# Norms of both MLPs and of the odd mixer summed row by row on ScalarE; their transposes and weight-sum transfers moved at the MLP entry

## The chip, the core and the metric

The kernel runs on one core of one Trainium2 chip. The metric is the device time of one execution in microseconds (us), as the median of several runs. The work is shared by TensorE (matmuls and transposes, PE below), VectorE (DVE), ScalarE (ACT), GpSimd (POOL), and the DMA queues that SyncE (SP) and GpSimd issue. TensorE writes its results into PSUM banks; `acc` names the banks of the projections and `aux` those of smaller jobs.

## The reference

A sequence of 512 rows with 1024 features goes through two layers, each a mixer and an MLP. Each of the four steps has its own RMS norm:

```python
def _rmsnorm(x, g):
    y = x * rsqrt(mean(x * x, axis=-1) + 1e-6)
    return y * g

def _mlp(x, g, w1, w2):                 # 1024 -> 4096 -> 1024
    return square(relu(_rmsnorm(x, g) @ w1)) @ w2

x = x + even_mixer(x)                   # window and neighbourhood attention
x = x + _mlp(x, ...)                    # "first MLP" below
x = x + odd_mixer(x)                    # q, k, v, g = rmsnorm(x) @ w_in; retention
x = x + _mlp(x, ...)                    # "second MLP" below
```

All inputs are float32.

## The kernel before, in words

**Products.** Every float32 operand of a matmul is split into a high and a low part (`whi`, `wlo` of a weight chunk, `xh`, `xl` of the residual times the norm's gain). A product is three matmuls: high by high, low by high, high by low; in a projection these are lines 177, 178 and 179 (`proj_a`) or 252 to 254 (`proj_b`). ScalarE casts the high part (line 158 for weights, 296 for the residual), VectorE subtracts for the low part (159 and 300). A chunk of weights holds four of the eight feature blocks, so a projection takes a new chunk at feature blocks 0 and 4.

**The residual.** It lies with features on the partitions, as eight tiles `xT` of 128 features by 512 rows. In the MLPs it is also wanted with rows on the partitions: `turn` transposes it (line 1346, 16 transposes of 128x128 for each half of the features) and ScalarE copies the result into the `rows` tiles. At the end of the first MLP `back` (line 1367) transposes it again, and `leave` copies it into `xT` for the odd mixer.

**The norm.** The norm's factor for a row of the sequence is applied behind the product, so a projection can start before the factor is known. The class `Norm` gets it so: ScalarE squares each `xT` tile (lines 321 and 324), the eight squares are added into `sqsum` (line 325, on GpSimd for the first MLP and the odd mixer, on VectorE for the second MLP), the sum is split into `sum_h` (cast, ScalarE, 339) and `sum_l` (VectorE, 340), and two matmuls with a tile of ones (341 and 342) sum over the partitions. `scales` then transposes the result `nv` into a column (four tiny transposes, line 1409) for the MLPs; `rows` and `cols` make from it the factor along the rows (`rstd_b`) for the q and k of the odd mixer and a column for its v.

**The MLP.** The second matmul of the MLP runs as a Strassen scheme, a hand-made schedule (`stream`) whose operands are sums of weight blocks. Its entry (`enter`) computes the first hidden blocks as four projections, called (0,0), (0,1), (1,0) and (1,1) below, 48 matmuls each. Between them stand other jobs: `scales`, `combine` (sums for the Strassen scheme from the residual), `ask` (which issues the transfers of the weight sums: a plain load on SP's queue, and where two blocks are to be added an accumulating transfer on GpSimd's queue, line 1099) and `turn`. The order of instructions on an engine is fixed when the kernel is built, and each engine runs its own in that order.

Of the kernel before, what the change touches and what calls it, by code (L numbers as in the profile page):

```python
# [32 lines left out]
def hybrid_encoder_kernel(  # L33
# [59 lines left out]
    rstd_c = consts.tile([P, 8], F32, name="rstd_c")  # L93

    consts.tile([P, 80], F32, name="filler")
# [66 lines left out]
    def proj_a(w, r0, nk, c0, xs, evac):  # L162
# [10 lines left out]
        for k, m in [(k, m) for k in range(nk) for m in range(2)]:  # L173
            hi, lo = weights(k - k % 4)
# [132 lines left out]
    class Norm:  # L307


        def __init__(self, vec):  # L310
            self.vec = vec
            self.xg = new_xg()
            self.sum = stat.tile([P, S], F32, tag="sqsum", name="sqsum")
            self.n = 0
# [4 lines left out]
        def square(self, d):  # L319
# [8 lines left out]
            self.n += 1  # L328

        def add(self, d):  # L330
            split_gain(self.xg[d], xT[d], self.gain(d))
            self.square(d)

        def squares(self):

            pb = aux()
            h = stat.tile([P, S], F32R, tag="rstd_b", name="sum_h")
            l = stat.tile([P, S], F32R, tag="sq", bufs=2, name="sum_l")
            nc.scalar.copy(h, self.sum)
            V.tensor_tensor(l, self.sum, h[:].bitcast(F32), op=ALU.subtract)  # L340
            mm(pb, ones_r, h, start=True, stop=False)
            mm(pb, ones_r, l, start=False, stop=True)
            v = stat.tile([P, S], F32, tag="sq", bufs=2, name="nv")
            V.tensor_scalar(v, pb, 1.0 / D, RMS_EPS, op0=ALU.mult, op1=ALU.add)
            return v

        def rows(self):

            v = self.squares()
            r = stat.tile([P, S], F32, tag="rstd_b", name="rstd_b")  # L350
            t = stat.tile([P, S], F32, tag="sq", bufs=2, name="nt")
            act(t, v, AF.Ln)
            act(r, t, AF.Exp, scale=-0.5)
# [1470 lines left out]
```

## Time and profile before

| what | value |
|---|---|
| runs | 1318.51, 1322.91, 1318.40 us; median 1318.51 us |
| profiled execution | 1322.95 us, of which the span is 1321.2 us |
| busy in the span | PE 1292.3 us (98%), DVE 1011.0 (77%), ACT 791.6 (60%), POOL 150.3 (11%) |
| DMA | 168.83 MB, 128 GB/s over the span |

The span is the time from the first to the last instruction that the profiler saw; the run's own time is 1.75 us longer. Busy is the sum of an engine's instructions. The times of the trace are counted from the span's start: the first MLP's entry runs from about 221 to 290 us, the odd mixer begins at about 566 us, the second MLP's entry at about 979 us. In a timeline the start of a matmul is followed by its duration; matmuls overlap, so what a matmul costs is the distance from one start to the next. In brackets stands how long the engine was idle before it, and which instruction released it.

### The profile page before, as it was taken

The page shows a single profiled execution, that of the slowest core. Times are in us where ns is not written, and L with a number is a line of the kernel's source. Part 1 is how long each engine was busy: PE and PEld are TensorE (multiplying, and loading weights), DVE is VectorE, ACT ScalarE, POOL GpSimd, SP SyncE. Part 2 cuts the span into 40 slices and gives each one's busy share as a digit, 9 for nine tenths or more (in the row PEclk, how much of TensorE's full clock was granted, in tenths as well). Part 3 has the DMA queues.
Part 4 walks back from the last instruction along what each step waited for, and adds up shares of the span by engine and source line. Part 5 has one row for each costly group of instructions (what it writes and reads, how often), then busy time and mean ns, then how long its engine had stood idle before and what let it go on. Part 6 is the DMA issues. An engine that isn't in the chain of part 4 may idle for free.

```text
span 1321.2 us, 18591 instructions
## 1 busy us (share of the span) xinstructions
PE 1292.3 (98%) x6954; PEld 1117.5 (85%) x6954; DVE 1011.0 (77%) x1568; ACT 791.6 (60%) x1308; POOL 150.3 (11%) x143
## 2 busy tenths in 40 slices
PE   7999999899999999999999999999999999999998
PEld 6888978688989989878888888888888889898997
DVE  5788887859797997976847647646678697979888
ACT  4789875665766757544645345345457657566573
POOL 0222431301011101030000000000000101101100
PEclk9999999999999999989999999999999999999999
DMA  5323322648688686232131332232236587867862
GB/s 167 86 78 89 99 65 80 183 125 199 175 197 199 163 203 177 65 95 94 49 96 48 96 96 64 80 96 80 64 97 191 140 200 185 194 170 176 219 152 80
DMA packets 147243, 168.83 MB, mean 128 GB/s; under 512 B 10817, under 2 KB 113233, under 8 KB 147153
## 3 DMA queue, kind: packets, MB, share of 16 engines
q1 hardware_dynamic: 120000, 134.89, 33.1%
q0 software_dynamic: 21408, 29.38, 13.7%
q10 hardware_dynamic: 5744, 3.37, 0.9%
q8 instruction: 55, 0.90, 0.3%
q14 instruction: 36, 0.29, 0.1%
HBM read 164.47 MB, written 3.15 MB: 127 GB/s over the span
## 4 chain that ended last, share of the span: by engine, by line
PE 89%; DVE 5%; ACT 2%; DMA 1%; POOL 1%; issue 1%; ACTq 0%; SPq 0%; DVEq 0%; POOLq 0%
PE acc L179 8%; PE acc L178 8%; PE acc L177 8%; PE acc L1338 7%; PE acc L1336 7%; PE acc L1337 7%; PE acc L1324 5%; PE acc L1325 5%; PE acc L1326 5%; PE acc L252 3%; PE acc L254 3%; PE acc L253 3%; PE aux L1634 1%; PE aux L1635 1%; PE aux L1636 1%; PE aux L1338 1%
## 5 line engine op out<-in xcount | busy, mean ns | idle before, releaser
L158 ACT CAST whi<-wraw 128x1024 fp32r<-128x1024 f32 (+2 forms) x115 | 112.0, 974 | 175.5 <-PE acc L178 89.9
L159 DVE TENSOR_TENSOR wlo<-wraw,whi 128x1024 fp32r<-128x1024 f32 (+2 forms) x106 | 123.4, 1164 | 92.1 <-ACT whi L158 90.7
L177 PE MATMUL acc<-xh,whi 128*128 128x512 f32 x400 | 157.5, 394 | 1.4 <-DVE xT L867 1.4
L178 PE MATMUL acc<-xl,whi 128*128 128x512 f32 x400 | 157.4, 393 | 0.3 <-DVE xl L300 0.3
L179 PE MATMUL acc<-xh,wlo 128*128 128x512 f32 x400 | 157.3, 393 | 0.0
L1128 ACT CAST whi<-sraw 128x1024 fp32r<-128x1024 f32 x94 | 98.6, 1051 | 66.1 <-PE acc L1338 27.8
L1134 DVE TENSOR_TENSOR wlo<-sraw,whi 128x1024 fp32r<-128x1024 f32 x94 | 114.9, 1222 | 20.1 <-ACT whi L1128 19.8
L1099 POOL DMA_DIRECT2D sraw<-in_w_mlp_out_dram x32 | 38.5, 1226 | 735.2 <-DMA sraw<-in_w_mlp_out_dram 510.8
L177 PEld LDWEIGHTS acc<-xh,whi 128*128 128x128 f32 x400 | 75.9, 190 | 17.8 <-DVE xT L867 1.8
L178 PEld LDWEIGHTS acc<-xl,whi 128*128 128x128 f32 x400 | 76.1, 190 | 16.2 <-DVE xl L300 0.7
L179 PEld LDWEIGHTS acc<-xh,wlo 128*128 128x128 f32 x400 | 75.9, 190 | 16.2 <-DVE wlo L159 0.2
L1324 PE MATMUL acc<-uh,whi 128*128 128x256 f32 x256 | 73.0, 285 | 0.2
L1325 PE MATMUL acc<-ul,whi 128*128 128x256 f32 x256 | 72.4, 283 | 0.0
L1326 PE MATMUL acc<-uh,wlo 128*128 128x256 f32 x256 | 72.4, 283 | 0.0
L1128 ACT CAST shi<-sraw 128x1024 fp32r<-128x1024 f32 x46 | 48.3, 1050 | 31.1 <-PE acc L1338 10.7
L1134 DVE TENSOR_TENSOR slo<-sraw,shi 128x1024 fp32r<-128x1024 f32 x46 | 56.2, 1222 | 9.2 <-ACT shi L1128 9.0
L252 PE MATMUL acc<-whi,xh 128*128 128x512 f32 x160 | 63.2, 396 | 0.0
L253 PE MATMUL acc<-wlo,xh 128*128 128x512 f32 x160 | 62.8, 394 | 0.0
L254 PE MATMUL acc<-whi,xl 128*128 128x512 f32 x160 | 62.7, 393 | 0.0
L202 PE MATMUL acc<-wlo,xh 128*128 128x384 f32 (+1 forms) x160 | 52.6, 329 | 0.0
L201 PE MATMUL acc<-whi,xh 128*128 128x384 f32 (+1 forms) x160 | 52.6, 331 | 0.0
L203 PE MATMUL acc<-whi,xl 128*128 128x384 f32 (+1 forms) x160 | 52.1, 327 | 0.0
(359 smaller groups left out, 3900.7 us busy)
## 6 DMA issues: line engine op xcount, KB each, us to landing
sraw<-in_w_mlp_out_dram SPq DMA_DIRECT2D x48, 512.0 KB
wraw<-in_w_in_o_dram SPq DMA_DIRECT2D x48, 512.0 KB
wraw<-in_w_mlp_in_dram SPq DMA_DIRECT2D x40, 512.0 KB
sraw<-in_w_mlp_in_dram SPq DMA_DIRECT2D x36, 512.0 KB
sraw<-in_w_mlp_out_dram POOLq DMA_DIRECT2D x32, 512.0 KB, 8.7
wraw<-in_w_mlp_out_dram SPq DMA_DIRECT2D x32, 512.0 KB
sraw<-in_w_mlp_in_dram POOLq DMA_DIRECT2D x24, 512.0 KB, 7.9
wraw<-in_w_out_o_dram SPq DMA_DIRECT2D x16, 512.0 KB
```

Of the source, the lines that this page charges most:

```text
L158: nc.scalar.copy(hu, used)
L159: eng.tensor_tensor(lu, used, hu.bitcast(F32), op=ALU.subtract)
L177: mm(ps[m], hi[:, k % 4, cs], xh, start=k == 0, stop=False)
L178: mm(ps[m], hi[:, k % 4, cs], xl, start=False, stop=False)
L179: mm(ps[m], lo[:, k % 4, cs], xh, start=False, stop=k == nk - 1)
L252: mm(o, lh, hi[:, k, :ncols], start=kb + k == 0, stop=False)
L1128: nc.scalar.copy(h, self.weight(k))
L1134: V.tensor_tensor(l, self.weight(k), h.bitcast(F32), op=ALU.subtract)
L1324: mm(o, h[:, i, cs], bh, start=st, stop=False, skip_group_check=True)
L1325: mm(o, h[:, i, cs], bl, start=False, stop=False, skip_group_check=True)
L1326: mm(o, l[:, i, cs], bh, start=False, stop=i == 3, skip_group_check=True)
L1338: mm(o, bl[:, i, cs], h[:, i], start=False, stop=end, skip_group_check=True)
```

## The change

The squares are taken from the `rows` tiles, which have the rows of the sequence on the partitions: `act(junk, rows, Square, accum_out=...)` is one ScalarE instruction that writes the squares to a place nobody reads and sums them along the row into one column of `tok_ss` (128 partitions, 4 blocks of rows, 2 halves of the features). So `sqsum`, its adds, the split, the two ones-matmuls and the transposes of `nv` are gone. `mean_square` adds the two halves and scales them (two VectorE instructions on 128x4). For the MLPs `scales` needs a reciprocal and a negation on 128x4 more. For the odd mixer a function `deviations`, called from the middle of the first q projection (before feature block 4), takes Ln and Exp on ScalarE and four refining VectorE instructions on 128x4, spreads the result over 128x512 (`wide`), transposes it four times (line 1489 of the kernel after) and copies it into `rstd_b`; v takes the column directly.

To have the rows early enough, `turn(0)` stands after projection (0,1) and `turn(1)` after (1,0), where they stood after (1,0) and after (1,1); `turn(1)`'s row copies, which were spread over the first four steps of `stream`, follow it at once. `scales` moves from after (0,0) to after (1,0). The first `ask` moves from after (0,0) to after (0,1), and the limits of the asks change.

```diff
-            if self.n == 0:
-                act(self.sum, xT[d], AF.Square)
-            else:
-                sq = stat.tile([P, S], F32, tag="sq", bufs=2, name="sq")
-                act(sq, xT[d], AF.Square)
-                (V if self.vec == V_MLP + 8 else G).tensor_tensor(
-                    self.sum, self.sum, sq, op=ALU.add
-                )
...
+    def mean_square():
+
+        v = tok_v
+        V.tensor_tensor(v, tok_ss[:, :, 0], tok_ss[:, :, 1], op=ALU.add)
+        V.tensor_scalar(v, v, 1.0 / D, RMS_EPS, op0=ALU.mult, op1=ALU.add)
+        return v
...
+        def square(self, t, half, junk):
+            act(junk, self.rows[t, half], AF.Square, accum_out=tok_ss[:, t, half : half + 1])
...
                     if (u, f) == (0, 0):
-                        self.scales()
                         self.combine(0)
                         self.combine(1)
-                        self.ask(-99, -8)
                     elif (u, f) == (0, 1):
                         self.combine(2)
-                        self.ask(-8, -5)
+                        self.turn(0)
+                        self.ask(-99, -6)
                     elif (u, f) == (1, 0):
                         self.combine(3)
-                        self.ask(-5, -2)
-                        copy = self.turn(0)
-                        for t in range(NB):
-                            copy(t)
+                        self.turn(1)
+                        self.ask(-6, -2)
+                        self.scales()
                         self.high(0)
                         self.low(0)
                     else:
                         self.ask(-2, 0)
-                        copy = self.turn(1)
-                        for k, t in enumerate((2, 3, 0, 1)):
-                            self.early.setdefault(k, []).append(lambda t=t: copy(t))
...
             for t in range(2):
                 self.square(t, 1, self.tmp())
             self.back(1)
...
+        def deviations():
+
+            rsqrt_small(rc, mean_square(), NB, tiny)
+            wide = stat.tile([P, S], F32, tag="sq", bufs=2, name="wide")
+            V.tensor_copy(
+                wide[:].rearrange("p (t m) -> p t m", t=NB),
+                rc.unsqueeze(2).to_broadcast([P, NB, P]),
+            )
+            pt = aux()
+            for t in range(NB):
+                ts = slice(t * P, (t + 1) * P)
+                nc.tensor.transpose(pt[:, ts], wide[:, ts], ident)
+            nc.scalar.copy(rb, pt)
```

How the instructions lie on the engines now, at the three places that matter. The names are tiles; the number behind `xh`, `xl` or `xT` tells one tile from another, and the line numbers of the kernel after differ from those of before (177 to 179 are 182 to 184, 300 is 305, 159 is 162, 1385 is 1351).

**First place: TensorE in the first MLP's entry.** Before, this is in the middle of projection (0,1); the other ones-matmul, of line 341, stands right ahead of that projection's first matmul:

```order
L177 MATMUL acc<-xh_2853,whi 128x512
L342 MATMUL aux<-sum_l,ones_r 128x512
L178 MATMUL acc<-xl_2854,whi 128x512
L179 MATMUL acc<-xh_2853,wlo 128x512
L177 MATMUL acc<-xh_2853,whi 128x512
L178 MATMUL acc<-xl_2854,whi 128x512
L179 MATMUL acc<-xh_2853,wlo 128x512
L177 MATMUL acc<-xh_2855,whi 128x512
L1409 MATMUL aux<-ident,nv 128x2 x4
L178 MATMUL acc<-xl_2856,whi 128x512
```

In the kernel after, projection (0,1) follows (0,0) with nothing between:

```order
L182 MATMUL acc<-xh_2865,whi 128x512
L183 MATMUL acc<-xl_2866,whi 128x512
L184 MATMUL acc<-xh_2865,wlo 128x512
L182 MATMUL acc<-xh_2851,whi 128x512
L183 MATMUL acc<-xl_2852,whi 128x512
L184 MATMUL acc<-xh_2851,wlo 128x512
L182 MATMUL acc<-xh_2851,whi 128x512
```

and behind the last matmul of (0,1) the transposes of `turn(0)` stand, 16 of them:

```order
L182 MATMUL acc<-xh_2865,whi 128x512
L183 MATMUL acc<-xl_2866,whi 128x512
L184 MATMUL acc<-xh_2865,wlo 128x512
L1310 MATMUL aux<-ident,xT_107 128x128
L1310 MATMUL aux<-ident,xT_108 128x128
L1310 MATMUL aux<-ident,xT_109 128x128
L1310 MATMUL aux<-ident,xT_110 128x128
L1310 MATMUL aux<-ident,xT_107 128x128
```

What moved: the two ones-matmuls and four transposes of `nv` are gone from projection (0,1), and the transposes of `turn` stand one projection (48 matmuls) earlier than before.

**Second place: TensorE in the odd mixer's first q projection.** Before, the q projection was complete and the next one had begun when the ones-matmuls came:

```order
L177 MATMUL acc<-xh_6056,whi 128x512
L178 MATMUL acc<-xl_6057,whi 128x512
L179 MATMUL acc<-xh_6056,wlo 128x512
L177 MATMUL acc<-xh_6042,whi 128x512
L341 MATMUL aux<-sum_h,ones_r 128x512
L178 MATMUL acc<-xl_6043,whi 128x512
L179 MATMUL acc<-xh_6042,wlo 128x512
L342 MATMUL aux<-sum_l,ones_r 128x512
L177 MATMUL acc<-xh_6042,whi 128x512
L178 MATMUL acc<-xl_6043,whi 128x512
```

In the kernel after, the second chunk's first products, a few of the next projection (`xh_6025` is its first feature block) and the low part of the second chunk come so:

```order
L182 MATMUL acc<-xh_6033,whi 128x512
L183 MATMUL acc<-xl_6034,whi 128x512
L182 MATMUL acc<-xh_6033,whi 128x512
L183 MATMUL acc<-xl_6034,whi 128x512
L182 MATMUL acc<-xh_6025,whi 128x512
L183 MATMUL acc<-xl_6026,whi 128x512
L182 MATMUL acc<-xh_6025,whi 128x512
L183 MATMUL acc<-xl_6026,whi 128x512
L184 MATMUL acc<-xh_6033,wlo 128x512 x2
L182 MATMUL acc<-xh_6035,whi 128x512
L183 MATMUL acc<-xl_6036,whi 128x512
```

and 14 matmuls behind the first one on `wlo` the spread factor is transposed:

```order
L182 MATMUL acc<-xh_6037,whi 128x512
L183 MATMUL acc<-xl_6038,whi 128x512
L184 MATMUL acc<-xh_6037,wlo 128x512
L1489 MATMUL aux<-ident,wide 128x128 x4
L182 MATMUL acc<-xh_6039,whi 128x512
L183 MATMUL acc<-xl_6040,whi 128x512
L184 MATMUL acc<-xh_6039,wlo 128x512
```

What moved: TensorE now wants the second chunk's `wlo` with matmuls of the next projection put ahead of it, and the factor (`wide`) one feature block before the q projection's end, where it wanted `sum_h` just behind that end.

**Third place: VectorE at the same time.** Before, the second chunk's `wlo` stood ahead of the last four `xl` and the last four copies into `xT`:

```order
L159 TENSOR_TENSOR wlo<-wraw,whi 128x1024
L300 SCALAR_TENSOR_TENSOR xl_6051<-aux,gv,xh_6050 128x512
L300 SCALAR_TENSOR_TENSOR xl_6053<-aux,gv,xh_6052 128x512
L300 SCALAR_TENSOR_TENSOR xl_6055<-acc,gv,xh_6054 128x512
L300 SCALAR_TENSOR_TENSOR xl_6057<-acc,gv,xh_6056 128x512
L1385 COPY xT_6144<-aux 128x512
L1385 COPY xT_6146<-aux 128x512
L1385 COPY xT_6148<-acc 128x512
L1385 COPY xT_6150<-acc 128x512
L1493 TENSOR_SCALAR ls_u<-hb 128x16
L1511 TENSOR_SCALAR gn<-gv 128x16
```

In the kernel after, the last four `xl` (not shown) and these copies stand ahead of it, and the small instructions of the factor are mixed with those of the decay (`ls_u`, `ls_s`, `ls_p`):

```order
L1351 COPY xT_6127<-aux 128x512
L1351 COPY xT_6129<-aux 128x512
L1351 COPY xT_6131<-acc 128x512
L1351 COPY xT_6133<-acc 128x512
L1449 TENSOR_SCALAR ls_u<-hb 128x16
L162 TENSOR_TENSOR wlo<-wraw,whi 128x1024
L1450 TENSOR_TENSOR ls_u<-ls_u,hb 128x16
L1467 TENSOR_SCALAR gn<-gv 128x16
L162 TENSOR_TENSOR wlo<-wraw,whi 128x1024
L1452 TENSOR_SCALAR ls_s_6145<-ls_u 128x16
L328 TENSOR_TENSOR tok_v<-tok_ss 128x4
L1453 RECIPROCAL ls_s_6145<-ls_s_6145 128x16
```

What moved: `wlo` of the second chunk from ahead of four `xl` and four copies to behind them.

SP's queue has six loads of the first layer's weights ahead of the first weight-sum loads, where it had five. The cast of the first weight-sum block on ScalarE (`shi`) stands ahead of the cast of the sixth weight chunk of the entry and ahead of projection (0,1)'s Relu, where it stood behind.

## Rows read from the trace of the kernel before

**Rows 1.** The page's chain that ended last, share of the span by engine.

```profile
PE 89%; DVE 5%; ACT 2%; DMA 1%; POOL 1%; issue 1%; ACTq 0%; SPq 0%; DVEq 0%; POOLq 0%
```

**Rows 2.** Waits of TensorE: us in total, times, longest.

```profile
PE aux L341 <- ACT sum_h L339: 5.5, 2, 3.2
PE aux L342 <- DVE sum_l L340: 3.1, 1, 3.1
```

**Rows 3.** TensorE's timeline, first MLP's entry: start, us, [idle before <-releaser].

```profile
231.17 0.50 PE L177 MATMUL acc<-xh,whi 128*128 128x512 f32 x1 [1.37 <-DVE xT L867]
...
240.92 0.50 PE L178 MATMUL acc<-xl,whi 128*128 128x512 f32 x1 [0.29 <-DVE xl L300]
...
247.42 0.50 PE L341 MATMUL aux<-sum_h,ones_r 128*128 128x512 f32 x1 [2.36 <-ACT sum_h L339]
...
254.07 0.80 PE L342 MATMUL aux<-sum_l,ones_r 128*128 128x512 f32 x1 [3.14 <-DVE sum_l L340]
...
255.09 0.63 PE L179 MATMUL acc<-xh,wlo 128*128 128x512 f32 x1
255.52 0.63 PE L177 MATMUL acc<-xh,whi 128*128 128x512 f32 x1
```

**Rows 4.** TensorE's groups from 220.9 to 289.75: busy us, mean ns.

```profile
L179 PE MATMUL acc<-xh,wlo 128*128 128x512 f32 x80 | 31.7, 397 | 0.0
...
L1346 PE MATMUL aux<-ident,xT 128*128 128x128 f32 x32 | 3.8, 272 | 0.0
```

**Rows 5.** VectorE's timeline, first MLP's entry.

```profile
224.92 0.75 DVE L300 SCALAR_TENSOR_TENSOR xl<-xT,gv,xh 128x512 fp32r<-128x512 f32 x1
...
239.09 1.78 DVE L300 SCALAR_TENSOR_TENSOR xl<-xT,gv,xh 128x512 fp32r<-128x512 f32 x1
```

**Rows 6.** GpSimd's timeline, first MLP's entry.

```profile
242.95 3.77 POOL L325 TENSOR_TENSOR sqsum<-sqsum,sq 128x512 f32<-128x512 f32 x1 [2.63 <-ACT sq L324]
```

**Rows 7.** Windows: PE, PEld, DVE, ACT, POOL busy; granted clock, DMA share, GB/s.

```profile
250.00:255.00 5.00, 1.86 (x7) 1.26 (x6) 5.00 (x9) 4.97 (x9) 0.00 (x0) 0.86 1.09 211
...
580.00:590.00 10.00, 7.83 (x22) 6.24 (x23) 6.96 (x23) 2.93 (x5) 1.38 (x2) 0.66 0.24 78
```

**Rows 8.** TensorE's timeline, odd mixer's entry.

```profile
582.17 0.79 PE L341 MATMUL aux<-sum_h,ones_r 128*128 128x512 f32 x1 [3.15 <-ACT sum_h L339]
...
595.52 0.39 PE L177 MATMUL acc<-xh,whi 128*128 128x512 f32 x1
...
596.20 0.39 PE L252 MATMUL acc<-whi,xh 128*128 128x512 f32 x1
```

**Rows 9.** TensorE's groups from 568.3 to 596.2.

```profile
L177 PE MATMUL acc<-xh,whi 128*128 128x512 f32 x31 | 13.0, 419 | 0.0
```

**Rows 10.** VectorE's timeline, odd mixer's entry.

```profile
569.79 1.22 DVE L159 TENSOR_TENSOR wlo<-wraw,whi 128x1024 fp32r<-128x1024 f32 x1
570.92 1.41 DVE L300 SCALAR_TENSOR_TENSOR xl<-aux,gv,xh 128x512 fp32r<-128x512 f32 x2
...
574.75 1.28 DVE L1385 COPY xT<-acc 128x512 f32<-128x512 f32 x2
...
577.56 1.26 DVE L1494 TENSOR_TENSOR ls_u<-ls_u,hb 128x16 f32<-128x16 f32 x1
...
586.43 0.17 DVE L1503 TENSOR_SCALAR ls_p<-ls_p 128x16 f32<-128x16 f32 x1
```

**Rows 11.** TensorE's timeline, second MLP's entry.

```profile
1004.91 0.39 PE L179 MATMUL acc<-xh,wlo 128*128 128x512 f32 x1
...
1011.61 0.40 PE L179 MATMUL acc<-xh,wlo 128*128 128x512 f32 x1
```

**Rows 12.** ScalarE's groups: busy us, mean ns.

```profile
L324 ACT ACTIVATE sq<-xT 128x512 f32<-128x512 f32 x21 | 13.0, 623 | 4.3 <-DVE ls_u L1494 1.8 <-DVE xT L1385 1.5 <-DVE ls_u L1493 0.9
...
L1583 ACT ACTIVATION_READ_ACCUMULATOR vr<-acc,rstd_c 128x1 f32 x32 | 6.2, 195 | 0.0
```

**Rows 13.** ScalarE's timeline, odd mixer's entry.

```profile
573.16 1.06 ACT L158 CAST whi<-wraw 128x1024 fp32r<-128x1024 f32 x1 [0.38 <-PE acc L178]
```

More of the change, by code (lines that the diff above doesn't have):

```diff
@@ L160, in load_w, with proj_a @@
         return hv, lv
[L162 removed]
+    def proj_a(w, r0, nk, c0, xs, evac, hook=None):
         ps = [acc(), acc()]
@@ L173, in proj_a @@
         for k, m in [(k, m) for k in range(nk) for m in range(2)]:
+            if hook is not None and (k, m) == (4, 0):
+                hook()
             hi, lo = weights(k - k % 4)
@@ L312, in __init__ @@
             self.xg = new_xg()
-            self.sum = stat.tile([P, S], F32, tag="sqsum", name="sqsum")
-            self.n = 0
         def gain(self, d):
             return gv[:, self.vec + d : self.vec + d + 1]
-        def square(self, d):
-            if self.n == 0:
-                act(self.sum, xT[d], AF.Square)
-            else:
-                sq = stat.tile([P, S], F32, tag="sq", bufs=2, name="sq")
-                act(sq, xT[d], AF.Square)
-                (V if self.vec == V_MLP + 8 else G).tensor_tensor(
-                    self.sum, self.sum, sq, op=ALU.add
-                )
-            self.n += 1
         def add(self, d):
             split_gain(self.xg[d], xT[d], self.gain(d))
[L332 to L353, printed above, removed]
-            V.tensor_tensor(t, v, r, op=ALU.mult)
-            V.tensor_tensor(t, t, r, op=ALU.mult)
-            V.scalar_tensor_tensor(t, t, 3.0, r, op0=ALU.subtract, op1=ALU.mult)
-            V.tensor_scalar(r, t, -0.5, None, op0=ALU.mult)
-            return r
-    def cols(row):
-        pc = aux()
-        for t in range(NB):
-            nc.tensor.transpose(
-                pc[:, 2 * t : 2 * t + 2], row[0:2, t * P : (t + 1) * P], ident[0:2, 0:2]
-            )
-        V.tensor_copy(rstd_c, pc[:, 0:8])
-        return rstd_c
+    def mean_square():
[3 more added lines that the diff above has]
+        return v
     def even_mixer(next_norm):
@@ L1262, in plan_second @@
             if q == 3 and not self.last:
+                for half, t in ((0, 0), (0, 1), (1, 2), (1, 3)):
+                    put(mid, s + 11 + half, lambda t=t, half=half: self.square(t, half, self.tmp()))
                 left = self.leave()
@@ L1351, in turn @@
                 tr.append(pt)
-            def copy(t):
+            for t in range(NB):
                 r = resid.tile([P, S], F32, tag=f"xT{4 * half + t}", name="rows")
@@ L1356, in copy @@
                 self.rows[t, half] = r
-            return copy
+                self.square(t, half, tr[t])
+        def square(self, t, half, junk):
+            act(junk, self.rows[t, half], AF.Square, accum_out=tok_ss[:, t, half : half + 1])
         def back(self, half):
@@ L1391, in leave @@
                 keep((d,))
+            for t in (2, 3):
+                self.square(t, 0, self.tmp())
             yield
@@ L1394, in leave @@
             keep((2, 3))
-            for d in range(3):
-                norm.square(d)
+            for t in range(2):
+                self.square(t, 1, self.tmp())
             self.back(1)
@@ L1400, in leave @@
             keep(range(4, 8))
[L1401 to L1402 removed]
         def scales(self):
[L1406 to L1413 removed]
+            v = mean_square()
+            self.r2, self.nr2 = tok_r[:, 0], tok_r[:, 1]
+            V.reciprocal(self.r2, v)
             V.tensor_scalar(self.nr2, self.r2, -1.0, None, op0=ALU.mult)
@@ L1562, in ev_q @@
                 def ev_q(m, ps):
-                    nonlocal rb
-                    rb = rb or norm.rows()
                     t = tmp()
```

32 lines of the change are left out of this document (12 added, 20 removed).

## The prediction

> **What bounds the kernel now.** I read the chain that ended last first: it lies on TensorE for 89% of the span [rows 1], so a microsecond (us) counts only if TensorE gets it back. The view of waits then says for what TensorE stands still: two of its longer entries are the norm's ones-matmuls [rows 2]. The timeline shows where. At the first MLP's entry it stops four times: 1.37 us for an `xT` add, 0.29 for an `xl`, 2.36 for `sum_h`, 3.14 for `sum_l` [rows 3], 7.16 us in all. At the odd mixer's entry it stops once, 3.15 us for `sum_h` [rows 8]. The second MLP's entry has no stop [rows 11]. Three matmuls start in 0.68 us where nothing disturbs them (595.52 to 596.20, [rows 8]), 0.2267 each; behind the stop at 254.07 the step from one start to the next is 0.43 [rows 3]. The windows say why: the granted clock is 0.86 in 250 to 255 and 0.66 in 580 to 590 [rows 7], that is, part of the time at the lower of TensorE's two levels, 1.2 in place of 2.4 GHz.
>
> So the change touches three places, and each is priced as a whole: the time that TensorE took there, less what its remaining matmuls take at 0.2267 us.
>
> **First MLP's entry, the largest term.** The stretch starts with a matmul at 220.8 (the last pieces of the even mixer's output) and ends where the Strassen stream starts at 289.48: 68.7 us. In it stand 80 matmuls of each of three lines and 32 transposes of `turn` [rows 4]. The matmuls take 240 x 0.2267 = 54.4 us. The transposes overlap: by the start of the first and of what follows them, 16 cost 1.7 us, so 3.4 for both turns; they stay, one projection earlier. The rest, 68.7 - 54.4 - 3.4 = **10.9 us**, is what could go: the 7.16 us of stops and 3.7 for the two ones-matmuls, four tiny transposes, restarts and the matmuls at the lower clock.
>
> Does each stop go? `sum_h` and `sum_l` exist no more, so the second pair goes for certain. The first pair was VectorE's: an `xl` takes 0.75 us alone and 1.78 when it starts behind one of GpSimd's adds (239.09 against 238.94, [rows 5, 6]), and `xT` and `xl` stand behind such stretched instructions. Without the adds VectorE is ahead of TensorE there by my walk along the new order, each instruction at its undisturbed duration. I take all 10.9; if the first pair stays in full, 9.2.
>
> What is added there lies on ScalarE and VectorE. The accumulating square isn't in the trace at this size. The plain one takes 0.62 us; the nearest accumulating instruction (v of the odd mixer) shows a separate read of the accumulator of 0.195 behind it [rows 12]. So one costs between 0.62 and 0.62 + 0.195 = 0.82; I take 0.75, nearer to the row that accumulates. Whether its unread result in a PSUM bank costs more than in SBUF, no row shows. Eight per norm replace eight squares and a cast; ScalarE gains or loses under 1 us. With the copies, a turn puts 4 x (0.62 + 0.75) = 5.5 us on ScalarE (a copy taken as long as the plain square), and has a projection of TensorE's, 48 x 0.2267 = 10.9 us, before the next turn wants its banks. The column arithmetic is four VectorE instructions on 128x4, 0.17 us each by the nearest tiny one [rows 10], and its result is wanted only by the stream, a projection later. All that at nothing; if the cover failed it would cost up to those 5.5 us.
>
> The transfers: one more 512 KB load stands ahead of the first weight sums, 2.5 us at the 211 GB/s that the busy window shows [rows 7]. The first sum's cast on ScalarE now stands ahead of the cast of the sixth weight chunk, which TensorE wants halfway through projection (1,0). With no stop, (0,0) starts at 220.8 + 10.9 = 231.7, (1,0) at 231.7 + 21.8 + 1.7 = 255.2, and the sixth chunk is wanted at 260.6. ScalarE and VectorE need 2.3 us for its parts (1.06 and 1.22, [rows 13, 10]), so a block that lands before about 257 (another 1.06 for its own cast) costs nothing. Before, ScalarE was 4.97 of 5 us busy in 250 to 255, with DMA at its limit [rows 7]; that is the rival below.
>
> **Odd mixer's entry.** From 568.30 to 596.20 [rows 8] there are 93 matmuls of three lines [rows 9]: 27.90 - 93 x 0.2267 = 6.8 us over. 3.15 is the stop, about 0.8 the ones-matmuls with restart; the rest, 2.8, is the lower clock. The change doesn't only remove. Three matmuls of the first projection are done by 568.30; with the other 21 of its first chunk TensorE is at 573.1, four later at 574.0 it takes the next projection's `whi`, whose cast ends at 574.2 [rows 13] (TensorE released it before, and does so at about the same time now), and at 575.1 it wants the second chunk's `wlo`. VectorE has to do four `xl` first, at 569.8 at the earliest (they started at 570.92 behind that `wlo` of 1.22, [rows 10]): 2 x 1.3 to 572.4, four copies (1.28 a pair) to 574.9, then a tiny one and `wlo`: 576.2. **A new wait of 1.1.** Fourteen matmuls later, at 579.4, TensorE wants `wide`. VectorE does another `wlo` to 577.6; two tiny instructions give the mean, Ln and Exp on ScalarE follow, then four refining ones which alternate with the decay's (eight at about 0.2) and the spreading copy of 0.64, as an `xT` copy [rows 10]. With about 0.5 for each of Ln and Exp with its hand-over (between a tiny VectorE instruction of 0.17 and a 128x512 square of 0.62) `wide` is ready at about 581.2. **A second new wait of 1.9.** Four transposes cost 0.5, a quarter of a turn with restart. Together 0.2 + 1.1 + 1.9 + 0.5 = 3.7, so the gain is 6.8 - 3.7 = **3.1 us**, if the clock stays up. Bounds: 6.3, if neither wait comes; -2.5, if the clock falls at both as it did before, at 2.8 each. One help: `ls_u`, 1.26 us beside GpSimd's add [rows 10], takes 0.17 without it. In the v projection four tiny transposes and their copy go: 0.3, between 0 and 0.8 (below).
>
> **Second MLP's entry.** From 1004.91 to 1011.61 are 24 matmul steps [rows 11]: 6.70 - 24 x 0.2267 = **1.3 us** for two ones-matmuls and four transposes; the matmuls alone are 0.45, the transposes with restart 0.8. VectorE loses seven adds; no stop here to win.
>
> **Sum.** 10.9 + 3.1 + 0.3 + 1.3 = 15.6 us off the profiled execution's own 1322.95: 1307.3, said as 1307. That execution is one of two at 1322.9, while two other runs are at 1318.4 and 1318.5, the median. If those two differ by TensorE's lower clock at the two stops (2.8 and part of the 3.7), it isn't there to be won in them, the gain is about 11, and the changed kernel takes 1307 all the same. If the 4.4 us lie elsewhere, its fast runs take 1303. What a measurement can tell from no change is about 0.5%, 6.6 us: faster is below 1311.9, slower above 1325.1.
>
> **A rule against it.** In this trace the stops of 3.14 and 3.15 us are followed by the lower clock, those of 1.37 and 2.36 are not [rows 3, 7, 8]; the new ones, at 1.1 and 1.9, would be like the latter. The Trainium skill, "TensorE: Matmul & The Clock Gate", section "HAM oscillation — how this bites in real kernels", tells of a kernel whose every wait between groups of matmuls brings the lower clock back, so that it is paid once for each wait. By that rule two short waits in place of one long one are worse, not better, and the sum would be 1313 in place of 1307. So far the rows bear it out only for the long stops.
>
> **Rivals.**
> - *The odd entry gives all back* (0.17). The clock falls at one or both new waits, or `wide` comes later. One fall: 3.1 - 2.8, time 1310; two: 15.6 - 5.6 = 10 us, time 1313. For it: two waits close together on one queue; against: the row just named. About a third of it is above 1311.9.
> - *ScalarE or a transfer stops TensorE at the first MLP's entry* (0.13). The first sum's cast holds the chunk cast, Relu and row copies behind it. For it: ScalarE and DMA are full at 250 to 255 [rows 7]; against: the casts of `combine` in that crowd were queued behind `sum_h`, and run earlier without it. About 5 us back (one turn's ScalarE work): 1312, between 1309 and 1317; half of it no measurable change.
> - *Slower* (0.04). The same cast, but its block lands far later because loads stand ahead of it. From 257 each us costs one; the gain is gone at 273, and over 275 the time passes 1325. Only a loss of 16 us in a queue whose extra load is 2.5 would do it.
> - *The stops are not the norm's* (0.06, within "no measurable change"). VectorE and ScalarE keep the entry as late for `combine` and casts, so the stop moves to the next `whi` or `wlo`: only the lower clock and removed matmuls go, about 4 + 1.3 us, time 1317.
> - *Better* (0.06): no new waits at the odd entry, and the 4.4 us elsewhere: 1300.
>
> The forecast itself, 1303 to 1310, has 0.54. Faster: 0.54 + 0.06 + 0.11 + 0.07 = 0.78; same: 0.18; slower: 0.04. The range is 1301 to 1314, which leaves out the last two rivals, the slower one and the tail of the second: about 0.2.
>
> **What would show it.** Right: in TensorE's timeline no stop between 231 and 260, the Strassen stream about 11 us earlier, no GpSimd add and no VectorE `xl` over 0.8 us; two waits at the odd entry, on `wlo` and `wide`, with steps of 0.23 behind them; no extra steps at the second MLP's entry. Wrong: a wait on `whi` or `wlo` in (0,1) or (1,0), a wait for a PSUM bank at the second turn, accumulating squares over 1 us, or a granted clock under 0.9 in the 10 us behind the odd entry's waits.

## The result and the profile after

| | median of five runs | lowest to highest |
|---|---|---|
| before | 1319.03 us | 1318.40 to 1322.91 |
| after | 1305.78 us | 1304.45 to 1305.87 |

The ratio is 0.9892, with a 95% interval from 0.9877 to 0.9907: 13.3 us less. One execution of before (1818.58 us, the one profiled as `before_again`) and one of after (2832.64 us, among the runs of `after_again`) took far longer than all others, so they are left out of every median below, and so is that profile. The profiled execution of after took 1304.45 us with a span of 1302.7, which is 18.5 us less than the span of before's profiled execution. The difference between 13.3 and 18.5 is that of the two executions that were profiled: before's was among its slowest (1322.95), after's was the quickest of its five.

TensorE's waits in the kernel after (engine, tile, line, who released it: us in total, times, longest). The first is the start of the kernel and was there before. No norm is in the list any more; the last two are the odd mixer's entry.

```profile
PE aux L353 <- DMA qk<-in_x_dram: 5.3, 2, 3.9
...
PE acc L184 <- DVE wlo L162: 0.4, 1, 0.4
...
PE acc L182 <- DVE xT L1351: 0.2, 1, 0.2
```

TensorE's timeline at the first MLP's entry: its first matmul, the two turns and the first matmul of the Strassen stream. None of the rows between them has a wait.

```profile
219.79 0.39 PE L182 MATMUL acc<-xh,whi 128*128 128x512 f32 x1
...
252.43 1.91 PE L1310 MATMUL aux<-ident,xT 128*128 128x128 f32 x16
...
265.08 1.91 PE L1310 MATMUL aux<-ident,xT 128*128 128x128 f32 x16
...
277.75 0.39 PE L1300 MATMUL acc<-shi,hB 128*128 128x512 f32 x1
```

From 219.79 to 277.75 are 57.96 us, where before took 68.68 [rows 3, 4]. The 240 matmuls and two turns take 54.4 + 3.4 = 57.8 by the prediction's figures, so nothing is left to gain there. The windows (PE, PEld, DVE, ACT, POOL busy, then granted clock, DMA share, GB/s) show TensorE busy throughout and the clock at its upper level; the last two rows, the odd mixer's entry and what follows it, answer to the row at 0.66 in [rows 7].

```profile
240.00:260.00 20.00, 20.00 (x98) 16.82 (x97) 14.09 (x26) 16.26 (x33) 2.45 (x2) 1.00 0.82 234
260.00:280.00 20.00, 20.00 (x98) 16.77 (x97) 9.85 (x18) 15.45 (x32) 2.41 (x2) 1.00 0.58 161
560.00:570.00 10.00, 9.40 (x41) 6.74 (x40) 9.68 (x37) 2.69 (x6) 0.00 (x0) 1.00 0.33 107
570.00:580.00 10.00, 10.00 (x46) 8.27 (x45) 8.92 (x16) 5.02 (x7) 0.00 (x0) 1.00 0.35 100
```

TensorE's timeline at the odd mixer's entry. It holds the two waits that the profile names, and the four transposes of `wide` with a gap of 0.15 us in front (the matmul at 567.35 would be followed after 0.23, at 567.58).

```profile
562.55 0.47 PE L182 MATMUL acc<-xh,whi 128*128 128x512 f32 x1 [0.19 <-DVE xT L1351]
...
564.27 0.73 PE L184 MATMUL acc<-xh,wlo 128*128 128x512 f32 x2 [0.41 <-DVE wlo L162]
...
567.35 0.39 PE L184 MATMUL acc<-xh,wlo 128*128 128x512 f32 x1
567.73 0.66 PE L1489 MATMUL aux<-ident,wide 128*128 128x128 f32 x4
568.15 0.47 PE L182 MATMUL acc<-xh,whi 128*128 128x512 f32 x1
...
579.61 0.39 PE L257 MATMUL acc<-whi,xh 128*128 128x512 f32 x1
```

VectorE at the same time: the last two copies into `xT`, the second chunk's `wlo`, the first and the last of the four refining instructions, and the copy that spreads the factor. Below them stand ScalarE's Ln and Exp for the factor.

```profile
561.73 1.28 DVE L1351 COPY xT<-acc 128x512 f32<-128x512 f32 x2
...
563.00 1.22 DVE L162 TENSOR_TENSOR wlo<-wraw,whi 128x1024 fp32r<-128x1024 f32 x1
...
566.42 0.16 DVE L116 TENSOR_TENSOR rq_t<-tok_v,rq_r 128x4 f32<-128x4 f32 x1
...
567.06 0.16 DVE L119 TENSOR_SCALAR tok_r<-rq_t 128x4 f32<-128x4 f32 x1
...
567.26 0.42 DVE L1482 COPY wide<-tok_r 128x512 f32<-128x512 f32 x1
```

```profile
565.94 0.20 ACT L112 ACTIVATE rq_l<-tok_v 128x4 f32<-128x4 f32 x1 [1.39 <-DVE tok_v L329]
566.18 0.20 ACT L114 ACTIVATE rq_r<-rq_l 128x4 f32<-128x4 f32 x1
```

At the second MLP's entry 24 matmul steps now take exactly 24 x 0.2267 = 5.44 us, where the same steps took 6.70 with the norm's instructions between them [rows 11]:

```profile
1004.04 0.39 PE L182 MATMUL acc<-xh,whi 128*128 128x512 f32 x1
...
1009.48 0.39 PE L182 MATMUL acc<-xh,whi 128*128 128x512 f32 x1
```

The accumulating square, in ScalarE's groups (busy us, mean ns of one, idle before): 0.62 us and 0.21 for the read of its accumulator. The two overlap: in ScalarE's timeline the next instruction starts 0.62 us behind the square.

```profile
L1324 ACT ACTIVATE aux<-rows 128x512 f32<-128x512 f32 x16 | 9.9, 623 | 0.0
...
L1324 ACT ACTIVATION_READ_ACCUMULATOR aux<-rows 128x1 f32 x16 | 3.4, 212 | 0.0
```

Laid stage by stage beside before, by the starts of the same matmuls in the two timelines, the 18.5 us are:

| stage | before | after | less by | predicted |
|---|---|---|---|---|
| up to the first MLP's entry | 220.8 | 219.8 | 1.0 | - |
| first MLP's entry, up to the stream | 68.7 | 58.0 | 10.7 | 10.9 |
| odd entry: last 156 matmuls of the stream, up to the first v matmul | 70.3 | 65.7 | 4.7 | 3.1 |
| v projection and first quarter's retention | 72.5 | 72.1 | 0.4 | 0.3 |
| second MLP's four projections | 142.5 | 141.3 | 1.2 | 1.3 |
| all else | | | 0.5 | - |

In the four places that were forecast 17.0 us went where 15.6 were counted. The 1.0 us in front of them is scatter: the kernel after reached this entry at 219.8 us in this execution and at 221.2 in that of `after_again`.

### The profile page after: what moved, and what is told of

The parts are those of the page before. It is cut to its first block, busy times and chain, and to the rows that moved or that the text cites. A ratio compares the mean times of both kernels' runs of the same rounds, so it can differ in the third digit from the quotient of the medians.

```text
span 1302.7 us, 18552 instructions
## 1 busy us (share of the span) xinstructions
PE 1284.1 (99%) x6940; PEld 1112.6 (85%) x6940; DVE 997.1 (77%) x1561; ACT 789.6 (61%) x1330; POOL 126.0 (10%) x129
## 3 DMA queue, kind: packets, MB, share of 16 engines
HBM read 164.47 MB, written 3.15 MB: 129 GB/s over the span
## 4 chain that ended last, share of the span: by engine, by line
PE 83%; DVE 7%; ACT 6%; issue 2%; DMA 1%; POOL 0%; ACTq 0%; SPq 0%; DVEq 0%
PE acc L184 9%; PE acc L182 9%; PE acc L183 9%; PE acc L1301 7%; PE acc L1300 7%; PE acc L1302 7%; PE acc L1288 3%; PE acc L1290 3%; PE acc L1289 3%; PE acc L257 3%; PE acc L259 3%; PE acc L258 3%; PE aux L1602 1%; PE aux L1603 1%; PE aux L1604 1%
## 5 line engine op out<-in xcount | busy, mean ns | idle before, releaser
L1257 DVE SCALAR_TENSOR_TENSOR rows<-acc,tok_r,rows 128x512 f32<-128x512 f32 (+1 forms) x97 | 71.5, 740 | 1.9 <-PE acc L1302 1.9
L1090 ACT CAST shi<-sraw 128x1024 fp32r<-128x1024 f32 x46 | 48.3, 1050 | 30.7 <-PE acc L1302 10.7
```

Of the source, the lines that this page charges most:

```text
L1090: nc.scalar.copy(h, self.weight(k))
```

## The experiments

Ratios are to the kernel before, run on the same chip beside it, with a 95% interval; us are medians. Where a stage is named, it is that of the table above.

**The kernel before, once more.** No edit.

> The kernel before, unchanged. Theory: the 4.4 us between its two kinds of executions (1318.5 and 1322.9) are TensorE's lower clock behind the two stops. If this execution takes about 1318.5 to 1319, the granted clock stays at 1.00 at 245 to 260 and at 580 to 590 us, with the same stops; if it takes 1322.9, the clock falls there again. Rival: the difference lies elsewhere (the first loads), and the clock falls at the stops in both kinds.

1320.06 us, ratio 1.0002 (0.9993 to 1.0012). The runs answer the question in part. In all, the kernel before took from 1317.0 to 1323.9 us in 48 runs, with no gap over 1.1 us, so there are no two kinds of executions, as I had read out of three runs. For 43 of them the mean granted clock is on record, and the time goes with it: the 9 runs at 0.996 took 1321.8 us on average, the 29 at 0.997 1319.9, the 5 at 0.998 or 0.999 1317.9. So a good part of the scatter is TensorE's lower clock. At which of the two stops it fell in each run isn't on record.

**One half of the change alone.** `mlp_only` has the MLPs' part: turns with squares, `scales`, the order in `enter`; the odd mixer's norm stays.

```diff
         def add(self, d):
             split_gain(self.xg[d], xT[d], self.gain(d))
-            self.square(d)
...
                 nc.scalar.copy(r, tr[t])
                 self.rows[t, half] = r
+                self.square(t, half, tr[t])
```

> Only the MLPs' norms, turns and asks of the change; the odd mixer's norm as before. Theory: the two MLP entries give their whole gain by themselves, 10.7 at the first (up to 2 less where the clock didn't fall) and 1.2 at the second: 1307 to 1310. The odd entry keeps its stop of about 3 us for the cast of the sum. Rival: the gains are not independent, and with GpSimd's adds of the odd norm still there part of the first is given back: 1312 or more.

1308.76 us, ratio 0.9916 (0.9900 to 0.9932), 11.0 us less. The first entry takes 58.0 us, as in the kernel after, the second MLP's projections 141.3. The odd entry keeps its stop:

```profile
571.48 0.50 PE L344 MATMUL aux<-sum_h,ones_r 128*128 128x512 f32 x1 [3.13 <-ACT sum_h L342]
```

`odd_only` has the other half: squares of the rows in `plan_second` and `leave`, and `deviations`.

```diff
-                    rb = rb or norm.rows()
...
-                proj_a(w_in_o, 0, 8, qt * 256, xg, ev_q)
+                hook = None if qt else deviations
+                proj_a(w_in_o, 0, 8, qt * 256, xg, ev_q, hook)
```

> Only the odd mixer's norm of the change; both MLPs as before. Theory: 4.7 us less at the odd entry and 0.4 in the v projection where the clock fell before, about 2.5 where it didn't: 1314 to 1317. Rival: the accumulating squares at the end of the Strassen stream hold ScalarE's casts up and take it back: 1318 to 1320.

1315.26 us, ratio 0.9963 (0.9949 to 0.9978), 4.5 us less: the odd entry takes 65.7 us, as in the kernel after. The halves are independent within the intervals: 0.9916 x 0.9963 = 0.9879, beside 0.9892 and 0.9887 for the whole. This execution also says something about the clock. At the first MLP's entry, unchanged here, TensorE stops for the same two reasons as before, and the windows show where the clock fell:

```profile
246.62 0.80 PE L347 MATMUL aux<-sum_h,ones_r 128*128 128x512 f32 x1 [2.35 <-ACT sum_h L345]
...
253.26 0.50 PE L348 MATMUL aux<-sum_l,ones_r 128*128 128x512 f32 x1 [1.72 <-DVE sum_l L346]
```

```profile
240.00:250.00 10.00, 7.54 (x26) 5.79 (x27) 7.45 (x16) 6.24 (x9) 6.16 (x3) 0.83 0.80 235
250.00:255.00 5.00, 3.28 (x14) 2.17 (x12) 5.00 (x9) 4.97 (x9) 0.00 (x0) 1.00 1.08 245
```

It fell behind the first stop, of 2.35 us, and not behind the second, of 1.72. In before's profile it was the other way round: not behind 2.36, but behind 3.14 [rows 3]. The entry took 67.3 us here, where it took 68.7 in before's profiled execution with the same work and order, so a gain at this place is 1.4 us smaller against this execution.

**What in the old norm cost the time.** `adds_dve` is the kernel before with one line changed.

```diff
-                (V if self.vec == V_MLP + 8 else G).tensor_tensor(
+                V.tensor_tensor(
                     self.sum, self.sum, sq, op=ALU.add
                 )
```

> The kernel before with the adds of the squares on VectorE for all three norms in place of GpSimd. Theory: the stops come from the chain of the sum itself, which has its cast and its split in the ordered queues: the stop for the low part of the sum at the first MLP's entry (3.1 us, behind the jobs of combine in VectorE's queue) stays, the stop for the cast shrinks, and seven adds of 0.69 us go onto VectorE: 1314 to 1319. Rival: GpSimd's slow adds and the VectorE instructions that they stretch are the whole cause; then all stops go and only ones-matmuls and transposes stay: 1308 to 1311.

1309.72 us, ratio 0.9919 (0.9900 to 0.9938), 10.0 us less from one changed line. My theory falls, and the time is the rival's; but the build also put other instructions in a new order, which is taken up below. The adds take 0.68 us on VectorE (the tile's row: minimum, median, maximum in ns, first and last start), where one of GpSimd's took up to 3.77 [rows 6]:

```profile
L325 DVE TENSOR_TENSOR sqsum<-sqsum,sq x21: 680/683/693, 228.0 to 985.2; 128x512 f32<-128x512 f32 x21
```

TensorE at the first entry and at the odd entry: the ones-matmuls are there, but of the four stops only 0.71 us is left, and at the odd entry 0.2 twice.

```profile
236.61 0.50 PE L177 MATMUL acc<-xh,whi 128*128 128x512 f32 x1 [0.71 <-DVE xT L867]
...
244.22 0.39 PE L341 MATMUL aux<-sum_h,ones_r 128*128 128x512 f32 x1
...
247.40 0.39 PE L342 MATMUL aux<-sum_l,ones_r 128*128 128x512 f32 x1
```

```profile
571.71 0.73 PE L179 MATMUL acc<-xh,wlo 128*128 128x512 f32 x2 [0.21 <-DVE wlo L159]
...
576.05 0.50 PE L341 MATMUL aux<-sum_h,ones_r 128*128 128x512 f32 x1 [0.20 <-ACT sum_h L339]
```

The first entry takes 60.1 us here (58.0 after, 68.7 before), the odd entry 65.5 (65.7 and 70.3). So beyond this one line the whole change is worth 2.2 us at the first entry, the 1.2 at the second MLP and 0.4 in the v projection; the rest of the gain is also had by taking the adds off GpSimd.

What the line alone did to the stop for `sum_l` isn't shown apart. In before `sum_l` stood behind two `ul` of `combine` in VectorE's queue (first fence); in `adds_dve` the build put it ahead of every `ul`, and the queue ran earlier as well (second fence).

```profile
246.75 0.62 ACT L339 CAST sum_h<-sqsum 128x512 fp32r<-128x512 f32 x1 [3.00 <-POOL sqsum L325]
...
248.03 0.43 DVE L1039 SCALAR_TENSOR_TENSOR c<-c,y 128x256 f32<-128x256 f32 x1 [2.43 <-ACT y L1033]
...
249.58 2.36 DVE L1045 TENSOR_TENSOR ul<-c,uh 128x1024 fp32r<-128x1024 f32 x2
...
253.33 0.68 DVE L340 TENSOR_TENSOR sum_l<-sqsum,sum_h 128x512 fp32r<-128x512 f32 x1
```

```profile
246.42 0.68 DVE L340 TENSOR_TENSOR sum_l<-sqsum,sum_h 128x512 fp32r<-128x512 f32 x1
247.03 1.22 DVE L1045 TENSOR_TENSOR ul<-c,uh 128x1024 fp32r<-128x1024 f32 x1
```

The first fence also shows how GpSimd's late sum reached `sum_l` in before: ScalarE waited 3.00 us for it with the cast of `sum_h`, the tile `y` of `combine` stood behind that cast on ScalarE, and VectorE waited 2.43 us for `y` with `sum_l` further back in its queue.

**By which path GpSimd's adds cost it.** They can cost by being slow in the norm's own chain, or by slowing VectorE beside them. `adds_dve_idle_pool` is `adds_dve` with fourteen GpSimd adds beside it that nobody waits for.

```diff
-                (V if self.vec == V_MLP + 8 else G).tensor_tensor(
-                    self.sum, self.sum, sq, op=ALU.add
-                )
+                V.tensor_tensor(self.sum, self.sum, sq, op=ALU.add)
+                if self.vec != V_MLP + 8:
+                    G.tensor_tensor(idle_sum, xT[d], xT[d], op=ALU.add)
```

> The kernel before with the sum's adds on VectorE, and fourteen GpSimd adds of the same size beside them that nobody waits for, for the first MLP and the odd mixer. With the adds on VectorE alone it was 1309.7. If the chain (sum late, cast late, low part late in VectorE's queue) was the cause of the long stops, it stays at 1310 to 1313, with only short stops behind stretched VectorE instructions. If the stretching is the cause, most comes back: 1315 to 1320. The order on the three engines changes in some 20 to 40 rows.

1317.30 us, ratio 0.9975 (0.9963 to 0.9987): 7.6 of the 10 us are back, at the first entry (64.1 us, 4.0 more than without) and at the odd entry (69.8, 4.3 more; the granted clock is 0.89 from 570 to 580 us and 0.94 from 580 to 590 there, so part of it is the lower clock behind the stop of 2.65 us at 578.5). TensorE now waits for VectorE's `wlo`, `xl` and `xT`, and for no sum:

```profile
PE acc L179 <- DVE wlo L159: 2.8, 2, 2.7
...
PE acc L178 <- DVE xl L300: 2.4, 2, 1.7
PE acc L177 <- DVE xT L867: 1.9, 2, 1.2
```

The order of some 20 to 40 rows on each of three engines differs from that of `adds_dve`, so not all of it need be the stretching. In `after_idle_pool` the order of the three engines is that of the kernel after: it is the kernel after with seven such adds at the first entry.

```diff
             split_gain(self.xg[d], xT[d], self.gain(d))
+            if d and self.vec != V_MLP + 8:
+                G.tensor_tensor(idle_sum, xT[d], xT[d], op=ALU.add)
```

> The kernel after with seven GpSimd adds of 128x512 at the first MLP's entry that nobody waits for (each adds an xT tile to itself into a tile that nobody reads); the order on TensorE, VectorE and ScalarE is unchanged. It parts two ways in which GpSimd's adds cost time before. If the adds cost because VectorE is stretched beside them (0.75 to 1.78 us for an xl), the two first stops of before come back, 1.4 + 0.3, and perhaps more behind them: 1307.5 to 1310. If they cost only because the norm's chain waited for them, nothing changes: 1304 to 1306.5.

1307.07 us, ratio 0.9901 (0.9886 to 0.9916), beside 0.9887 (0.9867 to 0.9907) for the kernel after: by the ratios alone, not clear of no change. The trace is clear: the first entry takes 60.2 in place of 58.0 us, and there is one stop, which isn't in the kernel after:

```profile
233.47 0.50 PE L184 MATMUL acc<-xh,wlo 128*128 128x512 f32 x1 [1.67 <-DVE wlo L162]
```

GpSimd and VectorE beside each other, a little later in that kernel: two adds from 237.40 on; an instruction on `c` of 0.94 us beside them, where the same instruction takes 0.41 alone at 242.90; two `xl` of 2.19, where a pair takes 1.41 alone in the kernel after (last fence).

```profile
237.40 2.22 POOL L325 TENSOR_TENSOR idle_sum<-xT 128x512 f32<-128x512 f32 x2 [3.09 <-DVE xT L831]
```

```profile
237.78 0.94 DVE L1002 TENSOR_TENSOR c<-y 128x256 f32<-128x256 f32 x1
238.64 2.19 DVE L305 SCALAR_TENSOR_TENSOR xl<-xT,gv,xh 128x512 fp32r<-128x512 f32 x2
...
242.90 0.41 DVE L1002 TENSOR_TENSOR c<-y 128x256 f32<-128x256 f32 x1
```

```profile
230.70 1.41 DVE L305 SCALAR_TENSOR_TENSOR xl<-xT,gv,xh 128x512 fp32r<-128x512 f32 x2
```

The Trainium skill, "SBUF — State Buffer", section "Who interferes with whom", says that a VectorE instruction with two inputs in SBUF and a GpSimd one that reads SBUF exclude each other, and whichever starts second is held up. The trace agrees in kind: 0.94 in place of 0.41 for such an instruction.

**The requests for the weight sums.** `asks_old` puts them where they were before, `asks_late` moves the first one projection further.

```diff
                     if (u, f) == (0, 0):
                         self.combine(0)
                         self.combine(1)
+                        self.ask(-99, -8)
                     elif (u, f) == (0, 1):
                         self.combine(2)
                         self.turn(0)
-                        self.ask(-99, -6)
+                        self.ask(-8, -5)
                     elif (u, f) == (1, 0):
                         self.combine(3)
                         self.turn(1)
-                        self.ask(-6, -2)
+                        self.ask(-5, -2)
```

> The kernel after with the requests for the weight sums at the places of before. Theory: the first block's cast on ScalarE came 12 us before TensorE needs anything behind it, so the place of the requests is worth nothing here: within 1 us of the kernel after. Rival: the earlier cast waits for its transfer and holds chunk casts and row copies behind it: 2 to 5 us slower, with a TensorE stop on a weight chunk in projection (0,1) or (1,0).

1305.22 us, ratio 0.9891 (0.9876 to 0.9906), beside 0.9887 (0.9867 to 0.9907) for the kernel after. This part of the change is worth nothing that can be measured.

```diff
                         self.turn(0)
-                        self.ask(-99, -6)
...
                         self.turn(1)
-                        self.ask(-6, -2)
+                        self.ask(-99, -2)
```

> The kernel after with the first request for the weight sums only behind projection (1,0). Theory: the first block then lands behind the point from which each us costs one; the loads are issued some 15 us later, ScalarE's cast of it holds the last chunk's cast, and TensorE stops for 3 to 10 us at projection (1,1) or the start of the stream, at both MLPs: 1309 to 1325. Rival: the transfers still hide: within 1 us of the kernel after.

1313.82 us, ratio 0.9955 (0.9940 to 0.9970): 8.2 us slower than the kernel after beside it (1305.61). The stop is at the stream's start, not in projection (1,1); the cast waits for the transfer, and TensorE for the cast and the low part.

```profile
278.38 1.04 ACT L1090 CAST shi<-sraw 128x1024 fp32r<-128x1024 f32 x1 [3.24 <-DMA sraw<-in_w_mlp_out_dram]
```

```profile
279.47 0.50 PE L1300 MATMUL acc<-shi,hB 128*128 128x512 f32 x1 [1.25 <-ACT shi L1090]
280.73 0.50 PE L1301 MATMUL acc<-slo,hB 128*128 128x512 f32 x1 [0.76 <-DVE slo L1096]
...
287.16 0.50 PE L1301 MATMUL acc<-wlo,hU 128*128 128x512 f32 x1 [0.65 <-DVE wlo L1096]
```

The first of these stops belongs to the entry (59.4 in place of 58.0 us). The stream's first 168 matmuls take 41.8 us in place of 38.1 at the first MLP and 41.6 at the second: TensorE waits again for the low parts of the blocks that follow, for 0.65 us at 287.16 and 0.58 at 293.70, with restarts.

**The kernel after, beside these.**

> The kernel after, unchanged, beside the next three: 1304 to 1306.

1305.61 us, ratio 0.9887 (0.9867 to 0.9907).

**The place of the turns.** `turns_old` (the copies and squares of `turn(1)` follow it at once, where in before its copies were spread over the stream's first steps):

```diff
                     elif (u, f) == (0, 1):
                         self.combine(2)
-                        self.turn(0)
                         self.ask(-99, -6)
                     elif (u, f) == (1, 0):
                         self.combine(3)
-                        self.turn(1)
                         self.ask(-6, -2)
-                        self.scales()
+                        self.turn(0)
...
                     else:
                         self.ask(-2, 0)
+                        self.turn(1)
+                        self.scales()
```

> The kernel after with both turns one projection later, where they stood before, and the scales behind the second. Theory: the move of the turns is what hides the copies and accumulating squares (eight instructions, 5.5 us of ScalarE for a turn); at the start of the stream they stand ahead of casts that are wanted every 2.7 us, and the first read of a product waits for the scale: 1 to 5 us slower for each MLP, 1307 to 1315. Rival: ScalarE has room there too: within 1 us of the kernel after.

1308.66 us, ratio 0.9915 (0.9901 to 0.9930), 3.1 us slower than the kernel after beside it. The entry itself takes as long; the stream's first 168 matmuls take 39.9 in place of 38.1 us at the first MLP and 40.0 at the second. One stop of 0.58 us is at the first casts behind the turn's copies and squares; two more steps onto a low part, at 286.55 and 293.29, take 0.49 and 0.51 us in place of 0.23, and the rest is restarts.

```profile
290.15 0.50 PE L1301 MATMUL acc<-wlo,hU 128*128 128x512 f32 x1 [0.58 <-DVE wlo L1096]
```

**What a square costs.** `squares_twice` does each accumulating square a second time.

```diff
             act(junk, self.rows[t, half], AF.Square, accum_out=tok_ss[:, t, half : half + 1])
+            act(junk, self.rows[t, half], AF.Square, accum_out=tok_ss[:, t, half : half + 1])
```

> The kernel after with each of the 24 accumulating squares done twice into the same places. Theory: a square with its accumulator read costs ScalarE 0.62 to 0.82 us and none of it is on the path: 1304.5 to 1307. Rival: ScalarE is near its limit at the MLP entries (8 more at each, 5 us), and chunk casts or Relus come late: 1309 to 1316.

1307.14 us, ratio 0.9900 (0.9885 to 0.9915), beside 0.9887 for the kernel after: 24 more squares, about 15 us of ScalarE at 0.62 from one start to the next, cost at most 1 to 2 us, just above the theory's range. Both MLP entries take as long as without them; the stream's first 168 matmuls take 38.8 in place of 38.1 us at each MLP.

**The order of the last copies.** `keep_order`:

```diff
-            keep(range(4, 8))
+            keep((6, 7, 4, 5))
```

> The kernel after with the last four copies into xT in the order 6, 7, 4, 5, so that the two acc banks which the next projection wants come free 1.2 us earlier. Theory: the wait for a bank at the odd entry (0.19 us with a restart of 0.15) goes, the wait for the second chunk's low part 1.7 us later takes its place by as much: no change that can be measured, 1304 to 1306.5. Rival: the bank set the pace of what followed, and some 0.5 us go.

1305.22 us, ratio 0.9887 (0.9872 to 0.9902). The wait for the bank is gone, and that for `wlo` grew from 0.41 to 0.7 us: no change, as expected. None of the kernels tried is faster than the kernel after by a measurable amount.

## Why the prediction was right, point by point

The forecast was 1307, between 1301 and 1314; 1305.78 was measured, and faster was the likeliest.

*First MLP's entry: right in size.* 10.7 us went, 10.9 were counted; all four stops are gone and no new one came. Counting stops, extra instructions and slow matmuls as a remainder against the undisturbed step gave the size without a price for each. That both pairs of stops end with the MLPs' part of the change is shown by `mlp_only`. But the text leaves open how much of it needs this change: in `adds_dve` 8.5 of the 10.7 are won by taking the adds off GpSimd and by the order that the build then chose, since the sum is ready before TensorE asks for it. I had expected there that the low part's place in VectorE's queue would keep the long stop. It didn't, but the experiment doesn't refute the reason, since that place changed too.

*The price of GpSimd's neighbourhood: seen, sized too small.* The prediction gave 1.7 us, the first pair of stops, to the stretched VectorE instructions. Seven idle adds cost the kernel after one stop of 1.67 us and 2.2 with restarts at this entry, and in `adds_dve`, where VectorE is fuller and the order shifts, 4.0. How the long stops divide between the slow chain and the stretching can't be settled exactly, since with the slow chain both come together.

*Odd entry: mechanism right, size off.* Of "0.2 + 1.1 + 1.9 + 0.5 = 3.7" the step that failed is the second new wait, 1.9 for `wide`: 0.15 us were measured in front of the transposes, 0.3 with the restart. The other terms came. TensorE started on the second chunk's `wlo` 7.85 us behind the matmul that answers to 568.30 (556.42 to 564.27), where the forecast had 7.9; over the 29 matmuls before it that is 1.3 us, as 0.2 + 1.1, though part of it was a wait for a bank that wasn't forecast (0.19, beside 0.41 for `wlo`, the rest restarts). The transposes with their restart cost 0.5. That makes 2.1 in place of 3.7, and a gain of 4.7 in place of 3.1. The 1.9 was too long in each of its parts: Ln and Exp started 0.24 us apart and not 0.5 (565.94, 566.18), the refining instructions and the decay's between them about 0.1 us apart and not 0.2 (seven from 566.42 to 567.06), and the spreading copy took 0.42 and not 0.64. So `wide` was ready at 567.7, as TensorE came to it. And the clock stayed up, as the forecast had it: 1.00 up to 580.

*v projection and second MLP: right*, 0.4 and 1.2 for 0.3 and 1.3.

*What was costed at nothing.* A square took 0.62 us of ScalarE from start to start, where 0.75 was taken. The squares are hidden, but not wherever they stand and not in any number: with the turns one projection later the same work costs 3.1 us (`turns_old`), and twice the squares cost 0.7 us at the start of each stream (`squares_twice`). The later requests for the weight sums are worth nothing (`asks_old`), and the rival that a late block stops TensorE is real, but has its price one projection further on (`asks_late`).

*The clock.* The step "the stops of 3.14 and 3.15 us are followed by the lower clock, those of 1.37 and 2.36 are not" reads one execution rightly, but not as a rule by length: in `odd_only` the clock fell behind 2.35 us. It did no harm, as the new waits are shorter still. The rule that the prediction set against itself was not put to the test, since no wait of 1.1 or 1.9 us came; that it would reach waits as short as those was the prediction's own reading. The Trainium skill, "TensorE: Matmul & The Clock Gate", section "What's actually happening", says that how many matmuls run slow at a kernel's start differs from run to run of one kernel. The two executions here agree in kind: with the same work and order up to this entry, the clock fell behind different stops. The reading of the 4.4 us between runs as two kinds of executions falls with the 48 runs; that the scatter is in good part the lower clock stands, by the granted clocks of 43 of them. So the sum was rightly taken off the profiled execution, which at 0.996 is one of those with the lowest clock; part of why the medians lie 13.3 us apart and not 17.0 is that most runs of before lost less to it.

## What to carry to other kernels

Price a place by what the bound engine took there less its remaining work at its undisturbed step; the remainder holds stops, restarts and slow matmuls at once, and came out within 0.2 us where nothing new was in the way. Before a chain is replaced, try the cheapest cause alone: here one line, the adds' engine, with the order that the build then chose, held three quarters of the gain. A GpSimd instruction that nobody waits for still costs if VectorE, beside it, feeds the engine that sets the end.

## What the runs showed of the hardware

- An accumulating ScalarE square of 128x512 takes 0.62 us and a read of its accumulator 0.21, and the next instruction starts 0.62 us behind the square; with the unread result in PSUM or in SBUF alike (0.62 and 0.63).
- A GpSimd add of 128x512, 0.68 us on VectorE, took up to 3.77 in the old norm, and 2.22 for two beside VectorE in `after_idle_pool`: both engines lengthen when they meet (an instruction on `c` there took 0.94 in place of 0.41).
- A VectorE copy that spreads four columns over 128x512 within SBUF took 0.42 us, a copy of that size out of PSUM 0.68.
- Whether TensorE's clock falls behind a stop of about 2.35 us is not the same in every execution: behind 2.35 in `odd_only` it fell, behind 2.36 in before's profile it didn't.
